# SSM exchange copied by GpSimd, SSM output written and loaded by halves, and other buffers for the FFN's first up weights

## The chip, the cores and the metric

The kernel runs on one core of a Trainium2 chip. What is measured is the device time of one execution, in microseconds (us); the time of a kernel is the median of its runs.

## The reference, cut to what matters

One layer of a hybrid encoder for a prompt of 1024 tokens and a sample of 64, width 1024. Both go through the same weights, so the kernel treats them as 1088 token columns.

```python
proj = rmsnorm(x) @ w_in                  # q, k, v, u, gate_attn, gate_ssm
o_attn = stick_breaking(q, k, v)          # 8 heads of 64
# S5: 32 groups of 16 channels, 64 complex states each
s[t] = lam * s[t-1] + B u[t];  y = Re(C s) + D u
y = gelu(y);  o_ssm = y * sigmoid(y @ w_glu)
merged = sigmoid(g_attn) * (o_attn @ w_branch_attn) + sigmoid(g_ssm) * (o_ssm @ w_branch_ssm)
x = x + rmsnorm(merged @ w_out)
f = (silu(f0 @ w_gate) * (f0 @ w_up)) @ w_down          # f0 = rmsnorm(x), 2816 wide
x = x + rmsnorm(f);  x = x + rmsnorm(sigmoid(rmsnorm(x) @ w_ple_gate) * (p @ w_ple_proj))
```

## The kernel before, in words

All products are made of split operands: a float32 matrix becomes a high part, rounded by a copy on ScalarE, and a low part, the difference on VectorE (`split` and `unit`, lines 106 to 126), and three matmuls make one product (lines 137 to 139).

The order on each engine and on each DMA queue is not written by hand here. The framework plans it from the order in which the program names its operations and from a simulated timeline (`schedule_with_timeline_sim=True`); on the chip each queue then runs strictly in that order. Nearly all DMAs are issued by SyncE (SP), a few by GpSimd.

**The SSM.** Time is cut into chunks of T = 8 steps: 128 chunks of the prompt, one empty column and 8 of the sample make NCH = 137 columns. Each group becomes two matmuls of 128x128 on 137 columns: a Toeplitz block `toep` on the inputs `ut` (line 571) and the table `cm` on the chunk states `hist` (line 572). Real and imaginary parts and the two halves of the groups lie on different halves of the partitions, so that `cm`, and later `hist`, has to be exchanged between partitions 0 to 63 and 64 to 127: `exchange` sends each half by DMA into `cx` (lines 542 and 543) and copies it back in place, one copy on ScalarE (line 544), one on VectorE (line 545). The chunk states come from a scan on VectorE, some hundred small steps (`cmul`, lines 271 to 277). `ssm_out` then does the matmuls of three groups into one bank, evicts it with a Gelu on ScalarE into `ut` (line 573), twelve evictions in all, the halves of the groups in turn. When all are done it writes `ut` to a DRAM tensor `ydr`, one DMA for each of the 8 steps (line 577), 16 partitions and 32 groups each. `glu` loads `ydr` back with the channels on the partitions, four tiles `y` of 128 channels (line 585), splits each into `ya`, and multiplies by `w_glu`, for each bank over k = 0, 1, 2, 3.

Beside the SSM TensorE has other work: the gate projections and parts of q, k and v (`fill`), which are made column by column in between, evicted by ScalarE (`gs`, line 909; two buffers) and stored to DRAM (line 910). Their weights are split at lines 119 and 115. In this stage the projections take three banks in turn.

**The FFN's start.** The FFN runs in 11 blocks of 256 columns. `wino_weights` loads two halves of a block's gate or up weights (line 1116) and splits them. For i even, the gate, the raw tile comes from the pool `W`, which is open all the time (tag `wraw`, two buffers); for i odd, the up weights, from the pool `ffn1`, tag `raw`, which is opened when the pool of the stage before (`mix`) is closed and lies over it. `ffn_first` treats block 0 in its own way: both weights are split first, and only their plain products are made (sums=False). Before it, `mix_out` finishes the tokens: a norm, transposes, and the stores of sums of token blocks to `tk` (line 1029), which `wino_tokens` loads again as `st` (line 1103).

The functions that the change touches, and what calls them:

Of the kernel before, what the change touches and what calls it, by code (L numbers as in the profile page):

```python
# [8 lines left out]
F32 = mybir.dt.float32  # L9
F32R = mybir.dt.float32r  # L10
BF = mybir.dt.bfloat16
AF = mybir.ActivationFunctionType
# [13 lines left out]
T = 8  # L26
NCH = SEQ // T + 1 + DEC // T
# [41 lines left out]
class Net:  # L69
# [464 lines left out]
                n = N // (2 * s)  # L534
                step(cols(b + s, 2 * s, n), cols(b, 2 * s, n), n, l)

    def exchange(self, x, T):

        nc, n = self.nc, x.shape[2] // 2
        for i, t in enumerate(T):  # L540
            v = x[:, :, i * n:(i + 1) * n]
            nc.sync.dma_start(t[64:], v[:64, 1])
            nc.sync.dma_start(t[:64], v[64:, 0])
            nc.scalar.activation(v[64:, 0], t[64:], AF.Copy)
            nc.vector.tensor_copy(v[:64, 1], t[:64])

    def ssm_out(self, Q, U):
        nc = self.nc
        V, hist = nc.vector, self.hist

        ps = self.ps.tile([128, 512], F32, name="tr", tag="tr")
        fin = Q.tile([16, 4, 128], F32, name="fin")
        fs = Q.tile([128, 4, 16], F32, name="fs")
        V.tensor_copy(fs[:, 0:2], hist[:, :, :, S0 - 1])
        V.tensor_copy(fs[:, 2:4], hist[:, :, :, NCH])
        X = [U.tile([128, T, NCH], F32, name="us", tag="us", bufs=2) for _ in range(2)]
        self.exchange(hist[:, :, :, :NCH], X)
        for i in range(4):
            nc.tensor.transpose(ps[:16, i * 128:(i + 1) * 128], fs[:, i], self.ident)
        V.tensor_copy(fin, ps[:16].rearrange("g (i s) -> g i s", i=4))  # L560
        for i, o in enumerate((4, 5, 8, 9)):
            nc.sync.dma_start(self.O[o][0, 0].rearrange("(h g) p -> g h p", h=2),
                              fin[:, i].rearrange("g (h p) -> g h p", h=2))
        self.ydr = self.dram.tile([512, T, NCH], F32, name="ydr")
        for g0 in [h * 16 + i for i in range(0, 16, 3) for h in range(2)]:
            w = min(3, 16 - g0 % 16)
            ps = self.ps.tile([128, 512], F32, name="z", tag="z")
            for j in range(w):
                h, g = divmod(g0 + j, 16)
                o = ps[:, j * NCH:(j + 1) * NCH]  # L570
                nc.tensor.matmul(o, self.toep[:, g0 + j].rearrange("p n c -> p (n c)"), self.ut[:, g0 + j], start=True, stop=False)
                nc.tensor.matmul(o, self.cm[:, h, g].rearrange("p n c -> p (n c)"), hist[:, h, g, :NCH], start=False, stop=True)
            nc.scalar.activation(self.ut[:, g0:g0 + w], ps[:, :w * NCH].rearrange("p (a n) -> p a n", a=w),
                                 AF.Gelu_apprx_tanh)
        dst = self.ydr.rearrange("(g c) t n -> t c g n", c=16)
        for t in range(T):
            nc.sync.dma_start(dst[t], self.ut[t * 16:(t + 1) * 16])

    def glu(self, P):

        nc = self.nc
        Y, YA, B = [], [], []
        for k in range(4):
            y = P.tile([128, T, NCH], F32, name="y", tag="y", bufs=4)
            nc.sync.dma_start(y, self.ydr[k * 128:(k + 1) * 128])
            ya = P.tile([128, 2, TOK], F32R, name="ya", tag="ya", bufs=4)
            for c0, n0, n in ((0, 0, SEQ // T), (SEQ, S0, DEC // T)):
                h, l = (ya[:, i, c0:c0 + n * T].rearrange("p (c t) -> p t c", t=T) for i in range(2))
                self.split(h, l, y[:, :, n0:n0 + n])
            Y.append(y)  # L590
            YA.append(ya)
        for m in range(4):
            s = P.tile([128, TOK], F32, name="sg", tag="sg", bufs=2)

            def evac(ci, c0, n, ps, s=s):
                nc.scalar.activation(s[:, c0:c0 + n], ps, AF.Sigmoid)
            self.fm_cols(self.I["w_glu"][0], m * 128, 4, evac, acts=YA)
            for c0, n0, n in ((0, 0, SEQ // T), (SEQ, S0, DEC // T)):
                v = s[:, c0:c0 + n * T].rearrange("p (c t) -> p t c", t=T)
                nc.vector.tensor_mul(v, v, Y[m][:, :, n0:n0 + n])  # L600
            if "o_ssm" in self.dbg:
                nc.sync.dma_start(self.dbg["o_ssm"][m * 128:(m + 1) * 128], s)
            b = P.tile([128, 2, TOK], F32R, name="bs", tag="bs", bufs=4)
            self.split(b[:, 0], b[:, 1], s)
            B.append(b)
        for m in range(8):
            g = P.tile([128, TOK], F32, name="gl", tag="gl", bufs=2)
            nc.sync.dma_start(g, self.gd[8 + m])

            def evac(ci, c0, n, ps, g=g):  # L610
                nc.vector.tensor_mul(g[:, c0:c0 + n], ps, g[:, c0:c0 + n])
            self.fm_cols(self.I["w_branch_ssm"][0], m * 128, 4, evac, acts=B)
            nc.sync.dma_start(self.gd[8 + m], g)
# [495 lines left out]
    def wino_weights(self, P, w, p, i, sums=True):  # L1109

        nc, W = self.nc, self.W
        G = nc.gpsimd
        raw, D = [], []
        for r in range(2):
            x = W.tile([128, 4, 256], F32, name="raw", tag="wraw", bufs=2) if i % 2 == 0 else P.tile([128, 4, 256], F32, "raw", "raw")
            nc.sync.dma_start(x, w[:, 4 * r:4 * r + 4, p * 256:(p + 1) * 256])
            if not sums and i == r == 1:
                h, l = (P.tile([128, 4, 256], F32R, n, "s") for n in ("wh", "wl"))
            elif (2 * i + r) % 3 < 2:
                h = W.tile([128, 4, 256], F32R, name="wh", tag="whi", bufs=2)  # L1120
                l = W.tile([128, 4, 256], F32R, name="wl", tag="wlo", bufs=2)
            else:
                h, l = P.tile([128, 4, 256], F32R, "wh", "dh"), P.tile([128, 4, 256], F32R, "wl", "dl")
            self.split(h, l, x)
            raw.append(x)
            D.append((h, l))
        if not sums:
            return D
        a11, a21 = (raw[0][:, :, s:s + 128] for s in (0, 128))
        a12, a22 = (raw[1][:, :, s:s + 128] for s in (0, 128))  # L1130

        def part(op, x, y):
            t = P.tile([128, 4, 128], F32, "st", "st")
            op(t, x, y)  # L1134
            s = P.tile([128, 2, 4, 128], F32R, "s", "s")
            self.split(s[:, 0], s[:, 1], t)
            return t, (s[:, 0], s[:, 1])
        _, s3 = part(G.tensor_sub, a11, a21)
        t1, s1 = part(G.tensor_add, a21, a22)
        t2, s2 = part(G.tensor_sub, t1, a11)  # L1140
        _, s4 = part(G.tensor_sub, a12, t2)
        h = lambda d, n: tuple(x[:, :, n * 128:(n + 1) * 128] for x in d)
        return D, dict(a11=h(D[0], 0), a12=h(D[1], 0), a22=h(D[1], 1), s1=s1, s2=s2, s3=s3, s4=s4)
# [327 lines left out]
def body(tc, I, O, dbg=None, upto=99):  # L1471
    with ExitStack() as ctx:
        N = Net(ctx, tc, I, O, dbg, upto)
        nc = tc.nc
# [3 lines left out]
        W = N.W = ctx.enter_context(tc.tile_pool(name="W", bufs=1))  # L1478
# [15 lines left out]
        def fill(n):  # L1494
            for _ in range(n):
                next(dense, None)

        def pool(name, side="left"):
            return tc.tile_pool(name=name, bufs=1, reuse_waits="tile", side=side)
# [6 lines left out]
        with pool("ssm") as PS:  # L1506
            with pool("tab") as PT:
                N.ssm_load(PT)
                for _ in range(4):
                    for x in two:  # L1510
                        next(x, None)
                PU = pool("u", "right")
                pu = PU.__enter__()
                N.u_proj(pu)
                with N.tc.issue_after(N.last_dve.ins), N.tc.issue_after(N.last_pool.ins):
                    N.ssm_tables(PS, PT)
                    N.ssm_chunks(PS)
                    N.ssm_response(PS, PT)
            with pool("toep") as P1:
                N.ssm_toeplitz(P1)  # L1520
                N.exchange(N.cm.rearrange("p r g n c -> p r g (n c)"), [P1.tile([128, 8, 128], F32, name=f"cx{i}") for i in range(2)])
                N.ssm_scan(pu)
                fill(3 * G1)
                N.ssm_out(P1, pu)
            PU.__exit__(None, None, None)
# [29 lines left out]
        with pool("wout", "right") as PW:  # L1555
            N.HS = PW.tile([128, 8, 2 * DEC], F32R, name="HS")
            with pools(tc, "mrgB", dict(braw=1, ga=2, gs=2)) as P:
                raw = mA[0].tile([128, TOK], F32, "braw", "braw")
# [46 lines left out]
```

## Time and profile before

| | us |
|---|---|
| median of 3 runs | 1780.83 (1775.21 to 1787.9) |
| profiled execution | 1778.77 |
| its span, from the first to the last instruction | 1776.6 |
| TensorE busy in the span | 1692.9 (95%) |
| VectorE, ScalarE, GpSimd busy | 1039.0, 733.5, 515.3 |

The span is what the trace covers; the execution's own time is a little longer. In the rows below, L and a number is a line of the kernel; PE is TensorE, ACT ScalarE, DVE VectorE, POOL GpSimd, SP SyncE. Times are from the span's start.

### The profile page before, as it was taken

Reading aid. Unit: us, or ns where it says so; the run is one execution under the profiler, and the core shown is the slowest. Engines: PE = TensorE matmul, PEld = TensorE weight load, DVE = VectorE, ACT = ScalarE, POOL = GpSimd, SP = SyncE. Lnnn points to the kernel's source line nnn. Section 1 sums busy time; section 2 is a strip of 40 time slices with the busy share of each in tenths; the row PEclk is TensorE's granted clock in tenths of the full one; section 3 lists DMA queues with packets and bytes.
Section 4 is the critical chain, followed back from the end, with each engine's and each line's share of the span. In section 5 each row is a group of like instructions: output and inputs, shape, how many; then the busy total and the mean of one; then the engine's idle time right before and its main releaser. Section 6 shows DMA issues by size and latency. Waiting matters only on the chain.

```text
span 1776.6 us, 24710 instructions
## 1 busy us (share of the span) xinstructions
PE 1692.9 (95%) x9092; PEld 1479.3 (83%) x9092; DVE 1039.0 (58%) x1581; ACT 733.5 (41%) x1357; POOL 515.3 (29%) x446
## 2 busy tenths in 40 slices
PE   8999897999999988899998999999999999999998
PEld 6999897988888877799786788888888887888886
DVE  6437735435776777767463655555655455445674
ACT  6431134124555555643343433343333344444542
POOL 2026100012322323224230444445444313001453
PEclk9999898999999999999999999999999999999999
DMA  8352534675343342147454444445444386655332
GB/s 283 95 147 64 120 89 149 216 213 137 88 101 101 83 118 83 60 143 239 143 172 148 132 149 133 160 132 187 151 149 139 125 288 215 197 189 166 107 113 89
DMA packets 220457, 258.23 MB, mean 145 GB/s; under 512 B 25888, under 2 KB 168336, under 8 KB 220320
## 3 DMA queue, kind: packets, MB, share of 16 engines
q1 hardware_dynamic: 219680, 255.20, 46.9%
q0 software_dynamic: 656, 1.44, 0.5%
q8 instruction: 72, 1.18, 0.3%
q14 instruction: 49, 0.40, 0.1%
HBM read 165.32 MB, written 76.51 MB: 136 GB/s over the span
## 4 chain that ended last, share of the span: by engine, by line
PE 73%; DVE 12%; DMA 7%; ACT 3%; issue 3%; SPq 1%; POOL 1%; DVEq 0%; POOLq 0%; ACTq 0%
PE pj L1200 13%; PE tr L1200 6%; PE pj L137 6%; PE pj L139 6%; PE pj L138 6%; PE z L1366 3%; DVE p L730 3%; PE z L1200 3%; PE pj L1366 3%; PE z L138 2%; PE z L139 2%; PE z L137 2%; PE tr L1366 2%; PE av L806 2%; PE tr L776 1%
## 5 line engine op out<-in xcount | busy, mean ns | idle before, releaser
L137 PE MATMUL pj<-H,wh 128*128 128x362 f32 (+3 forms) x648 | 217.7, 336 | 5.9 <-DVE ql L629 3.3
L139 PE MATMUL pj<-H,wl 128*128 128x362 f32 (+3 forms) x648 | 215.1, 333 | 0.6 <-DVE wl L115 0.6
L138 PE MATMUL pj<-H,wh 128*128 128x362 f32 (+3 forms) x648 | 214.6, 331 | 0.0
L126 DVE TENSOR_TENSOR wl<-raw,wh 128x1024 fp32r<-128x1024 f32 x96 | 132.3, 1380 | 120.0 <-ACT wh L125 118.7
L732 POOL TENSOR_TENSOR w<-w,p 128x383 f32<-128x383 f32 (+4 forms) x68 | 92.7, 1372 | 312.5 <-DVE w L734 185.2
L125 ACT ACTIVATE wh<-raw 128x1024 fp32r<-128x1024 f32 x96 | 101.4, 1059 | 122.8 <-PE z L1366 45.5
L137 PEld LDWEIGHTS pj<-H,wh 128*128 128x128 f32 x648 | 122.8, 190 | 7.6 <-DVE ql L629 3.7
L139 PEld LDWEIGHTS pj<-H,wl 128*128 128x128 f32 x648 | 122.5, 189 | 1.5 <-DVE wl L115 0.8
L138 PEld LDWEIGHTS pj<-H,wh 128*128 128x128 f32 x648 | 122.7, 189 | 0.9 <-issue 0.4
L1200 PE MATMUL pj<-H,s 128*128 128x512 f32 x480 | 118.2, 395 | 0.0
L148 POOL TENSOR_TENSOR rs<-rs,mhalf 128x1 f32<-128x1 f32 (+1 forms) x54 | 32.6, 605 | 278.0 <-DVE rs L147 277.9
L1200 PEld LDWEIGHTS pj<-H,s 128*128 128x128 f32 x480 | 89.9, 188 | 21.0 <-DVE c L1233 0.3
L125 ACT ACTIVATE s<-st 128x512 fp32r<-128x512 f32 x80 | 50.3, 629 | 123.6 <-PE pj L1200 112.2
L1134 POOL TENSOR_TENSOR st<-raw 128x512 f32<-128x512 f32 x40 | 60.7, 1518 | 133.8 <-DVE H L126 54.0
L126 DVE TENSOR_TENSOR s<-st,s 128x512 fp32r<-128x512 f32 x80 | 67.8, 849 | 39.4 <-ACT s L125 38.7
L119 ACT ACTIVATE wh<-raw 128x1024 fp32r<-128x1024 f32 (+1 forms) x52 | 46.8, 899 | 94.2 <-PE av L138 48.8
L780 ACT ACTIVATE wth<-tr 128x512 fp32r<-128x512 f32 (+2 forms) x112 | 50.2, 454 | 82.4 <-PE tr L776 41.9
L781 DVE TENSOR_TENSOR wtl<-tr,wth 128x512 fp32r<-128x512 f32 (+2 forms) x112 | 55.3, 496 | 49.3 <-ACT wth L780 48.9
L115 DVE TENSOR_TENSOR wl<-raw,wh 128x1024 fp32r<-128x1024 f32 (+1 forms) x50 | 51.1, 1021 | 55.0 <-ACT wh L119 54.9
L728 ACT ACTIVATE p<-z 128x512 f32<-128x512 f32 (+4 forms) x116 | 59.1, 510 | 42.6 <-PE z L830 16.7
L730 DVE TENSOR_TENSOR_SCAN p<-p,zero 128x384 f32<-128x384 f32 (+4 forms) x68 | 73.9, 1094 | 0.2
L1200 PE MATMUL pj<-H,wh 128*128 128x512 f32 x224 | 72.7, 401 | 0.6 <-ACT H L125 0.4
(553 smaller groups left out, 4630.2 us busy)
## 6 DMA issues: line engine op xcount, KB each, us to landing
sd<-c SPq DMA_DIRECT2D x77, 256.0 KB, 3.2
raw<-sd SPq DMA_DIRECT2D x77, 256.0 KB, 2.9
raw<-in_w_in_dram SPq DMA_DIRECT2D x32, 512.0 KB, 5.3
raw<-in_w_ffn_gate_dram SPq DMA_DIRECT2D x22, 512.0 KB, 3.6
raw<-in_w_ffn_up_dram SPq DMA_DIRECT2D x22, 512.0 KB, 5.1
wd<-in_w_ffn_down_dram SPq DMA_DIRECT2D x44, 256.0 KB, 3.3
td<-wd SPq DMA_DIRECT2D x22, 512.0 KB, 3.2
raw<-td SPq DMA_DIRECT2D x44, 256.0 KB, 3.0
```

The lines of the kernel that those rows point to most:

```text
L125: self.nc.scalar.activation(wh, raw, AF.Copy)
L126: self.nc.vector.tensor_sub(wl, raw, wh)
L137: self.nc.tensor.matmul(out, wh, xh, start=i == 0, stop=False)
L138: self.nc.tensor.matmul(out, wh, xl, start=False, stop=False)
L139: self.nc.tensor.matmul(out, wl, xh, start=False, stop=i == n - 1)
L728: nc.scalar.activation(p, z, AF.Sigmoid, scale=-1.0)
L730: nc.vector.tensor_tensor_scan(p[:, ::-1], p[:, ::-1], self.zero.to_broadcast([128, n]), 1.0 if carry is None else carry, op0=OP.mult, op1 ...
L732: (nc.gpsimd if e == 'g' else nc.vector).tensor_tensor(w[:, :n - 1], w[:, :n - 1], p[:, 1:], op=OP.mult)
L781: nc.vector.tensor_sub(wl[:, a:b], ps[:, a:b], wh[:, a:b])
L1134: op(t, x, y)
L1200: self.nc.tensor.matmul(out, a[i][:, k], b[j][:, k], start=start and k == i == j == 0, stop=stop and k == 3 and i == 1, skip_group_check=n ...
L1366: nc.tensor.matmul(B[b + n], x[:, 0, c], y[:, 1], start=new and p == j == 0, stop=p == 10 and j == 2, skip_group_check=not new)
```

## The change

Three things are changed. The exchange of `cm` gets both copies on GpSimd (the exchange of `hist` stays on ScalarE and VectorE). `ssm_out` works through the first 8 groups of each half and then the last 8, six evictions each, and after each six it writes what it has: 16 DMAs, for each step and each half of the groups, of 16 partitions and 8 groups; `glu` loads and splits the tiles in the order 0, 2, 1, 3 (0 and 2 hold the first part), and uses them in the order 0, 1, 2, 3 as before. And the raw tile of block 0's up weights comes from `W` with the gate's.

```diff
-    def exchange(self, x, T):
+    def exchange(self, x, T, engines=None):
...
+        e = engines or (nc.scalar.copy, nc.vector.tensor_copy)
...
-            nc.scalar.activation(v[64:, 0], t[64:], AF.Copy)
-            nc.vector.tensor_copy(v[:64, 1], t[:64])
+            e[0](v[64:, 0], t[64:])
+            e[1](v[:64, 1], t[:64])
...
-        for g0 in [h * 16 + i for i in range(0, 16, 3) for h in range(2)]:
-            w = min(3, 16 - g0 % 16)
...
-        dst = self.ydr.rearrange("(g c) t n -> t c g n", c=16)
-        for t in range(T):
-            nc.sync.dma_start(dst[t], self.ut[t * 16:(t + 1) * 16])
+        dst = self.ydr.rearrange("(h b g c) t n -> b t c h g n", h=2, b=2, c=16)
+        src = self.ut.rearrange("p (h b g) n -> p h b g n", h=2, b=2)
+        for b in range(2):
+            for i in range(0, 8, 3):
+                for h in range(2):
+                    w = min(3, 8 - i)
+                    g0 = h * 16 + b * 8 + i
...
+            for t in range(T):
+                for h in range(2):
+                    nc.sync.dma_start(dst[b, t, :, h], src[t * 16:(t + 1) * 16, h, b])
...
-        for k in range(4):
+        for k in (0, 2, 1, 3):
...
-            x = W.tile([128, 4, 256], F32, name="raw", tag="wraw", bufs=2) if i % 2 == 0 else P.tile([128, 4, 256], F32, "raw", "raw")
+            x = W.tile([128, 4, 256], F32, name="raw", tag="wraw", bufs=2) if i % 2 == 0 or not sums else P.tile([128, 4, 256], F32, "raw", "raw")
...
-                N.exchange(N.cm.rearrange("p r g n c -> p r g (n c)"), [P1.tile([128, 8, 128], F32, name=f"cx{i}") for i in range(2)])
+                N.exchange(N.cm.rearrange("p r g n c -> p r g (n c)"), [P1.tile([128, 8, 128], F32, name=f"cx{i}") for i in range(2)],
+                           [nc.gpsimd.tensor_copy] * 2)
```

## Rows read from the trace of the kernel before

**Rows 1.** TensorE's timeline: start, us, engine, line, names, shapes, count, idle before and releaser.

```profile
199.59 0.67 PE L137 MATMUL av<-H,wh 128*128 128x362 f32 x1 [7.25 <-ACT gs L909]
...
281.88 0.67 PE L137 MATMUL tr<-ya,wh 128*128 128x364 f32 x1 [9.02 <-ACT ya L125]
```

**Rows 2.** TensorE's waits from 935 to 1010: us in total, times, longest.

```profile
PE tr L1200 <- ACT wh L125: 4.9, 1, 4.9
```

**Rows 3.** Windows: us, busy by engine (xcount), granted clock, DMA share, GB/s.

```profile
185.00:190.00 5.00, 5.00 (x32) 5.00 (x31) 0.71 (x4) 0.00 (x0) 0.00 (x0) 1.00 1.08 172
...
200.00:205.00 5.00, 5.00 (x18) 5.00 (x18) 4.66 (x17) 0.47 (x1) 0.00 (x0) 0.50 0.68 206
...
280.00:285.00 5.00, 2.31 (x6) 1.84 (x7) 3.14 (x3) 5.00 (x5) 0.00 (x0) 0.50 1.03 413
285.00:290.00 5.00, 5.00 (x24) 5.00 (x24) 5.00 (x6) 4.98 (x7) 0.00 (x0) 0.74 0.35 131
...
960.00:965.00 5.00, 4.95 (x15) 4.00 (x16) 4.58 (x6) 3.42 (x6) 0.00 (x0) 0.66 0.55 179
```

**Rows 4.** ScalarE's timeline around the exchange of cm.

```profile
190.37 1.06 ACT L544 ACTIVATE cm<-cx 64x1024 f32<-64x1024 f32 x1 [9.42 <-DMA cx<-cm]
...
199.08 0.46 ACT L909 ACTIVATE gs<-av 128x362 f32<-128x362 f32 x1
```

**Rows 5.** VectorE's timeline there: its two copies of the exchange.

```profile
190.36 0.68 DVE L545 COPY cm<-cx 64x1024 f32<-64x1024 f32 x1 [4.58 <-DMA cx<-cm]
...
197.05 0.69 DVE L545 COPY cm<-cx 64x1024 f32<-64x1024 f32 x1 [5.25 <-DMA cx<-cm]
```

**Rows 6.** Timelines of GpSimd and VectorE: a GpSimd copy and steps beside it.

```profile
154.50 2.16 POOL L430 COPY cbd<-dc 64x512 f32<-64x512 f32 x2
...
154.53 1.65 DVE L276 TENSOR_TENSOR us<-us 128x1024 f32<-128x1024 f32 x1
156.22 1.52 DVE L277 TENSOR_TENSOR hist<-hist,us 128x1024 f32<-128x1024 f32 x1
...
162.32 1.22 DVE L277 TENSOR_TENSOR hist<-hist,us 128x1024 f32<-128x1024 f32 x1
```

**Rows 7.** The same two timelines in the FFN: a GpSimd operation with two inputs.

```profile
1002.40 1.62 POOL L1134 TENSOR_TENSOR st<-raw,st 128x512 f32<-128x512 f32 x1
...
1002.79 1.78 DVE L1255 TENSOR_TENSOR c<-c 128x512 f32<-128x512 f32 x1
...
1006.19 0.68 DVE L1256 TENSOR_TENSOR c<-c 128x512 f32<-128x512 f32 x1
```

**Rows 8.** SP's queue: writes and loads of the SSM's output, loads of its input.

```profile
257.73 12.78 SPq L577 DMA_DIRECT2D ydr<-ut  x8
...
275.58 2.02 SPq L585 DMA_DIRECT2D y<-ydr  x4
...
90.58 5.41 SPq L484 DMA_DIRECT2D ut<-udr  x8
...
102.51 3.63 SPq L484 DMA_DIRECT2D ut<-udr  x8
```

**Rows 9.** ScalarE's timeline: the sixth and the last eviction, first splits of ya.

```profile
249.39 0.52 ACT L573 ACTIVATE ut<-z 128x411 f32<-128x411 f32 x1 [0.89 <-PE z L572]
...
257.42 0.29 ACT L573 ACTIVATE ut<-z 128x137 f32<-128x137 f32 x1 [0.28 <-PE z L572]
...
279.79 4.04 ACT L125 ACTIVATE ya<-y 128x1024 fp32r<-128x1024 f32 x3 [3.22 <-DMA y<-ydr]
```

**Rows 10.** DMA issues: names, queue, count, KB each, median us to landing.

```profile
ut<-udr SPq DMA_DIRECT2D x32, 68.5 KB, 3.2
```

**Rows 11.** ScalarE's timeline at the FFN's start: the first split of up weights.

```profile
958.94 1.06 ACT L125 ACTIVATE wh<-raw 128x1024 fp32r<-128x1024 f32 x1 [6.88 <-DMA raw<-in_w_ffn_up_dram]
```

**Rows 12.** SP's queue: the loads of the first gate and up weights.

```profile
849.52 8.85 SPq L1116 DMA_DIRECT2D raw<-in_w_ffn_gate_dram  x4
...
953.06 1.41 SPq L1116 DMA_DIRECT2D raw<-in_w_ffn_up_dram  x2
```

More of the change, by code (lines that the diff above doesn't have):

```diff
@@ L564, in ssm_out @@
         self.ydr = self.dram.tile([512, T, NCH], F32, name="ydr")
-        for g0 in [h * 16 + i for i in range(0, 16, 3) for h in range(2)]:
-            w = min(3, 16 - g0 % 16)
[L567 to L574, printed above, removed]
-        dst = self.ydr.rearrange("(g c) t n -> t c g n", c=16)
-        for t in range(T):
-            nc.sync.dma_start(dst[t], self.ut[t * 16:(t + 1) * 16])
+        dst = self.ydr.rearrange("(h b g c) t n -> b t c h g n", h=2, b=2, c=16)
[5 more added lines that the diff above has]
+                    g0 = h * 16 + b * 8 + i
+                    ps = self.ps.tile([128, 512], F32, name="z", tag="z")
+                    for j in range(w):
+                        o = ps[:, j * NCH:(j + 1) * NCH]
+                        g = b * 8 + i + j
+                        nc.tensor.matmul(o, self.toep[:, g0 + j].rearrange("p n c -> p (n c)"), self.ut[:, g0 + j], start=True, stop=False)
+                        nc.tensor.matmul(o, self.cm[:, h, g].rearrange("p n c -> p (n c)"), hist[:, h, g, :NCH], start=False, stop=True)
+                    nc.scalar.activation(self.ut[:, g0:g0 + w], ps[:, :w * NCH].rearrange("p (a n) -> p a n", a=w),
+                                         AF.Gelu_apprx_tanh)
+            for t in range(T):
+                for h in range(2):
+                    nc.sync.dma_start(dst[b, t, :, h], src[t * 16:(t + 1) * 16, h, b])
     def glu(self, P):
         nc = self.nc
-        Y, YA, B = [], [], []
-        for k in range(4):
+        Y, YA, B = [None] * 4, [None] * 4, []
+        for k in (0, 2, 1, 3):
             y = P.tile([128, T, NCH], F32, name="y", tag="y", bufs=4)
@@ L589, in glu @@
                 self.split(h, l, y[:, :, n0:n0 + n])
-            Y.append(y)
-            YA.append(ya)
+            Y[k], YA[k] = y, ya
         for m in range(4):
```

## The prediction

> **What bounds the kernel now.** I read the page first: TensorE is busy 95% of the span, so only stretches where it stands still, or runs at its lower clock, are worth anything. The list of TensorE's waits, stage by stage, comes next, and its timeline where the list has a long one. Around the SSM there are two: 7.3 us for an eviction of the gate projections (ACT gs), up to 199.59, and 9.0 us for the first split of the SSM's output (ACT ya), up to 281.88 [rows 1]. At the start of the FFN one stands out, 4.9 us for a weight split (ACT wh) [rows 2]. The windows table then shows what each costs behind itself: TensorE's granted clock is 1.00 (2.4 GHz) before the first of them and 0.50 (1.2 GHz) in the five us after it, with 18 matmuls where 32 of the same kind fit; 0.50 and 0.74 after the second; 0.66 after the third [rows 3]. Last, the timelines of the queues that stand in front of the three waits. Each part of the change touches one of them.
>
> **Part 1: the table's exchange on GpSimd.** Now ScalarE and VectorE each hold, in order, two copies of cm that wait for a DMA from another half of the partitions. ScalarE waits 9.42 us ahead of the first; the gate eviction due behind it runs only at 199.08 [rows 4], so TensorE runs out of banks. VectorE waits 4.58 and 5.25 us and copies for 0.68 and 0.69 [rows 5]: 11.2 us, and all of it is in the SSM's scan, whose small steps stand behind the copies.
> Removed for TensorE: 7.3 us of standing still, and the low clock after it, (32 - 18) x 5/32 = 2.2 us [rows 1, 3]: 9.5 us. Removed for the scan: 11.2 us. The matmuls of the SSM's output need both, so the smaller counts.
> Added: four copies of 64x1024 on GpSimd. The nearest row is its copy of 64x512, two in 2.16 us [rows 6], so one of 1024 is 2.16 us and the four 8.6 us. GpSimd has nothing else there: its busy time is 0.00 in the stretches on both sides [rows 3], and nothing is queued behind that would be needed soon. The table is first read by the SSM's output matmuls; of their twelve evictions the sixth runs at 249.39, 50 us behind the copies [rows 9], which is the cover; without it the four copies would add their 8.6 us.
> They do meet VectorE. While the two 64x512 copies ran, a VectorE step of 128x1024 took 1.65 us and the one behind it, half beside them, 1.52; soon after, without them, such a step took 1.22 [rows 6]. That is 0.73 us of VectorE for 2.16 us of GpSimd, so 2.9 us for 8.6. The other end is a GpSimd operation with two inputs: during one of 1.62 us a VectorE step took 1.78 us instead of 0.68 [rows 7]; at worst VectorE stands for all 8.6 us. I take 2.9, from the row that is a copy as well.
> So the scan gains 11.2 - 2.9 = 8.3 us (2.6 at worst), TensorE's own side 9.5; the part gives **8.3 us**, 2.6 to 9.5.
> The Trainium skill's page SBUF — State Buffer (Summary: rules for kernel authors) speaks against this part: a VectorE instruction with two SBUF inputs and a GpSimd one that reads SBUF block each other fully. The two-input rows agree with it, the copy rows show a third of it; by that rule this part would give 2.6 us.
> A store of gate columns that is issued behind the cx transfers will still land late. I cost that at nothing: an eviction has two buffers, and TensorE three banks of 24 matmuls each, 11 us at 32 in 5 us [rows 3]; that cover gone, TensorE would wait again, which the bounds hold.
>
> **Part 2: the SSM's output by halves.** The matmuls and Gelus now run to 257.7; only then are eight writes issued, in 12.78 us, and the loads of y start at 275.58; the first split runs at 279.79 [rows 8, 9]. TensorE resumes at 281.88, at half clock [rows 1]. From 280 to 290 it does 6 + 24 matmuls [rows 3]; at full speed, 0.156 us each, 30 matmuls would have ended at 290 had they begun at 285.3. That is the mark to compare with.
> After the change everything up to the Gelus is 8.3 us earlier. The first half is done after the sixth of twelve evictions, 249.91 - 8.3 = 241.6, the second at 249.4 [rows 9]. The writes are then 32 of 68.5 KB. Operations of just this shape and size are in the trace, the loads of ut: eight issues took 5.41 and 3.63 us (the other two sets lie between), 0.45 to 0.68 each, and a landing takes 3.2 us [rows 8, 10]. I take 0.55. The first sixteen go out by 241.6 + 8.9 = 250.5, beside the second half's matmuls; the next sixteen by 259.3; landed 262.5. The load of y takes 4.2 us (275.58 to 279.79), the split 1.06 on ScalarE [rows 11] and about 1.2 on VectorE. glu's matmuls take k in the order 0, 1, 2, 3, and k = 1 is of the second half: its first part is there at 262.5 + 4.2 + 1.1 = 267.8.
> TensorE has filling work until its wait begins; that was 9.0 us ahead of 281.9, at 272.9 [rows 1], and becomes 264.6, to which the nine matmuls of k = 0 add 1.4. It waits 1.8 us, and I add 1 for VectorE's part and the clock. Equivalent start: 267.8 - 1.4 + 1 = 267.4.
> One thing is not shown by the trace: the order on SP. The loads of y 0 and 2 wait for the first half's writes to land. Placed ahead of the second half's writes they hold them, and the column stores queued with them, for the 3.2 us of a landing and two more issues, and the longer wait costs clock: about 5 us, a start at 272.4. Which one the planner chooses can't be read from before; I take the middle, 270.
> Parts 1 and 2 together: 285.3 - 270 = **15.3 us**, between 12.9 and 17.9 by SP's order, and down to 7 with part 1 at its worst. The reordering of k among the loads costs nothing: the same splits, all before k = 1.
>
> **Part 3: the up weights.** The gate's two loads run at 849.52, and with them those of the next block's gate weights, four in all, because their buffers come from the pool that is open all the time. The first up weights have buffers of a pool that lies over the one before it: they are issued at 953.06, behind the stores of the last tokens, and split at 958.94 [rows 11, 12]. TensorE waits 4.9 us for that split [rows 2].
> With the gate's buffers the loads can go out where the next block's gate loads went, and land about 90 us early. The price: those gate loads come after the up splits, but they are needed only after all of the first block's products. The split still needs room in the pool that opens there, so it can't be as early as the load.
> Removed: 4.9 us and the clock, (1 - 0.66) x 5 = 1.7 us [rows 3]: 6.6 us. If the split's own room is late, nothing. The token loads behind the up loads start at the same stores as before, so a little may come back: I take **6 us**, 0 to 6.6.
>
> **The sum.** 15.3 + 6 = 21.3. The profiled execution took 1778.77 us, 2.2 of them outside its span: 1757.5. It lies 2.1 us below the median of the three runs, so I say 1758. The stages between and after are bound by TensorE, so the shift passes through.
>
> **The rivals.**
> - *GpSimd takes VectorE's time.* The scan gains 2.6, SP holds the second half: 12.9 - 5.7 = 7.2, with part 3 13.2: 1766. For it: rows 7. Against: rows 6, and that VectorE's steps there are short. 0.16.
> - *The up weights' split is late anyway*, for its room or its place on ScalarE: 1778.8 - 15.3 = 1763.5. For it: the row shows only that the load came last, not when the room was free. Against: ScalarE stands idle ahead of it. 0.14.
> - *Slower: a write costs by its count, not by its bytes.* SP took 1.6 us for each of the eight writes [rows 8]. If that were the price of an issue, 32 take 51 us: 241.6 + 51.1 + 3.2 + 4.2 + 1.1 = 301.2, 16 us behind the mark of 285.3; with part 3's 6 back, 10 us slower: 1789. It decides from about 1.2 us an issue. Against: the loads of ut, 0.45 to 0.68. 0.05.
> The page DMA: Bandwidth & Descriptors of the Trainium skill (Anatomy of one DMA — SWDGE (gpsimd) path) gives each DMA about 2.0 us whatever its size; one behind the other 32 would be an estimated 64 us. The ut rows speak against paying that in series.
> - *The change doesn't do what it says:* the planner writes every queue anew, the up loads stay behind the token stores, or an early split of y stands on ScalarE ahead of an eviction, as the cm copies did. Part of the 21 us then comes back as another wait: 1766 to 1780. 0.12.
>
> **How the numbers follow.** The forecast has 0.53, with its own range 1751 to 1764 (part 1 at 9.5, SP's better order and 6.6 make about 1753). All these cases but the slower one lie between 1750 and 1780; leaving out some of the fourth and the slower one, and keeping the median's own scatter below, the range is 1747 to 1776. About 1% (17.8 us, so 1763) is what a measurement of this kernel can tell from no change. The forecast is nearly all beyond it, the first two rivals a few us on this side of it: faster 0.58, same 0.37; slower by 1% needs the third rival and a replanned queue: 0.05.
>
> **What would show it.** Right: no wait of TensorE for gs near 192 and a clock of 1.00 through 200; the copies of cm on GpSimd, VectorE's scan without its two holes; the last Gelu at about 249 instead of 257; writes of ydr in two runs, the first beside the matmuls; TensorE's wait for ya at most 5 us; the up loads where four gate loads are now, and no wait for wh at the FFN's start. Wrong: VectorE steps lengthened to 2 us beside GpSimd; writes at over 1 us an issue; loads of y between the two runs of writes; ScalarE standing for y with evictions behind it; another wait of like length a few us after one that is gone.

## The result, and the profile after

The changed kernel takes 1769.57 us (median of 9 runs, 1766.16 to 1772.19), the kernel before 1781.46 beside it: ratio 0.9924, 95% interval 0.991 to 0.9938, some 13.5 us. The gain is clear of noise, under 1%, and smaller than the forecast: 1758 was said, 1747 to 1776 was the range.

The list of TensorE's waits around the SSM, after:

```profile
PE tr L560 <- DVE fs L556: 3.1, 1, 3.1
PE tr L138 <- DVE ya L126: 2.3, 2, 1.4
PE tr L560 <- DVE fs L555: 1.6, 1, 1.6
PE tr L137 <- ACT ya L125: 0.3, 1, 0.3
```

Both waits of [rows 1] are gone: none for gs, and ya is down from 9.0 us to 0.3 for ScalarE's part, while VectorE's part of it went from 0.8 us to 2.3. What has grown is the wait for the transposes of the final states (fs), which stand in TensorE's queue and need the scan. Before, it was 1.6 us:

```profile
PE tr L559 <- DVE fs L555: 1.6, 1, 1.6
```

After, it is 3.1 and 1.6 us, and the granted clock, 1.00 in the five us ahead, is down with it (columns as in [rows 3]):

```profile
220.00:225.00 5.00, 2.67 (x10) 2.59 (x11) 4.55 (x24) 0.00 (x0) 0.00 (x0) 0.62 0.38 127
225.00:230.00 5.00, 5.00 (x24) 5.00 (x23) 0.53 (x1) 1.06 (x1) 0.00 (x0) 0.70 0.69 151
```

GpSimd's timeline, and VectorE's beside it:

```profile
186.67 1.05 POOL L545 COPY cm<-cx 64x1024 f32<-64x1024 f32 x1 [8.25 <-DMA cx<-cm]
187.77 1.04 POOL L546 COPY cm<-cx 64x1024 f32<-64x1024 f32 x1
188.76 4.89 POOL L461 DMA_DIRECT2D toep<-kd  x8
193.69 1.93 POOL L545 COPY cm<-cx 64x1024 f32<-64x1024 f32 x1
195.67 1.66 POOL L546 COPY cm<-cx 64x1024 f32<-64x1024 f32 x1
```

```profile
186.63 0.22 DVE L271 TENSOR_TENSOR us<-hist,sq 128x32 f32<-128x32 f32 x1
186.76 1.03 DVE L272 TENSOR_TENSOR us<-hist,sqi 128x32 f32<-128x32 f32 x1
187.83 1.05 DVE L276 TENSOR_TENSOR us<-us 128x32 f32<-128x32 f32 x1
...
194.69 1.78 DVE L271 TENSOR_TENSOR us<-hist,sq 128x512 f32<-128x512 f32 x1
196.40 0.96 DVE L555 COPY fs<-hist 128x32 f32<-128x32 f32 x1
```

The copies take 5.7 us in all, 1.05 and 1.04 in the first pair, 1.93 and 1.66 in the second, which meets larger VectorE steps. The two small steps beside the first pair take 1.03 and 1.05 us where their neighbour takes 0.22. The planner also put the first pair ahead of the eight issues of toep, so these wait with GpSimd for cx. The queue of SP, before and after, shows what comes out: the exchange of hist, which ends the scan, starts 8.3 us earlier. (About 0.5 us of it is there ahead of the exchange of cm: a gate eviction that starts at 180.47 before starts at 179.96 after.)

```profile
233.29 0.63 SPq L542 DMA_DIRECT2D us<-hist  x1
```

```profile
224.97 0.63 SPq L543 DMA_DIRECT2D us<-hist  x1
...
241.02 8.40 SPq L583 DMA_DIRECT2D ydr<-ut  x16
...
250.14 7.62 SPq L583 DMA_DIRECT2D ydr<-ut  x16
...
260.61 2.17 SPq L591 DMA_DIRECT2D y<-ydr  x4
```

The writes go out in two runs, 0.53 and 0.48 us an issue; all four loads of y stand behind both, at 260.61 against 275.58 [rows 8]. The first sigmoid of glu, on ScalarE, is a mark that both kernels have. Before:

```profile
292.39 0.48 ACT L596 ACTIVATE sg<-tr 128x364 f32<-128x364 f32 x1 [2.06 <-PE tr L139]
```

and after:

```profile
278.45 0.48 ACT L601 ACTIVATE sg<-tr 128x364 f32<-128x364 f32 x1 [3.28 <-PE tr L139]
```

13.9 us earlier. So parts 1 and 2 came nearly as forecast; the rest is at the FFN's start. TensorE's waits there, after:

```profile
PE z L1196 <- DVE y L1193: 8.9, 1, 8.9
...
PE tr L1205 <- DVE wl L126: 0.3, 1, 0.3
```

The 4.9 us for wh [rows 2] are gone, and 8.9 us for y stand in their place, the input of the transposes of the sample's gated rows. That wait was there before too, in the line below the one in [rows 2]:

```profile
PE z L1191 <- DVE y L1188: 2.8, 1, 2.8
```

The windows of that stretch after (columns as in [rows 3]):

```profile
960.00:965.00 5.00, 0.00 (x0) 0.00 (x0) 2.62 (x4) 1.89 (x3) 0.00 (x0) 0.68 0.70 226
965.00:970.00 5.00, 1.51 (x5) 1.20 (x6) 2.81 (x6) 2.93 (x6) 0.00 (x0) 0.50 0.75 223
```

TensorE does nothing for these five us, and its granted clock is 0.68 in them and 0.50 in the next five. SP's queue and ScalarE's timeline show why:

```profile
843.53 2.73 SPq L1121 DMA_DIRECT2D raw<-in_w_ffn_up_dram  x2
...
945.04 0.93 SPq L1121 DMA_DIRECT2D raw<-in_w_ffn_up_dram  x2
946.02 1.29 SPq L1121 DMA_DIRECT2D raw<-in_w_ffn_gate_dram  x2
948.01 10.59 SPq L1108 DMA_DIRECT2D st<-tk  x5
```

```profile
937.42 2.01 ACT L125 ACTIVATE wh<-raw 128x1024 fp32r<-128x1024 f32 x2
...
956.24 1.94 ACT L125 ACTIVATE T<-st 128x512 fp32r<-128x512 f32 x3 [5.30 <-DMA st<-tk]
961.14 1.30 ACT L125 ACTIVATE T<-st 128x512 fp32r<-128x512 f32 x2 [2.96 <-DMA st<-tk]
963.08 0.63 ACT L125 ACTIVATE T<-st 128x512 fp32r<-128x512 f32 x1 [0.64 <-DMA st<-tk]
965.66 1.28 ACT L125 ACTIVATE T<-st 128x512 fp32r<-128x512 f32 x2 [1.94 <-DMA st<-tk]
966.84 0.36 ACT L978 ACTIVATE q<-av 64x256 f32<-64x256 f32 x1
```

The up loads go out at 843.53 and are split at 937.42 as the change wants. But q, the first step from the sample's product to its transposes, is queued on ScalarE behind the splits of the token sums (T), and each of those waits for its load. Counted from the first load of token sums (954.93 before, 943.65 after), TensorE came to the transposes after 25.9 us before and after 15.9 in the changed kernel, but y was ready after 28.7 and 24.8: TensorE gained 10 us on that load, y only 4.

### The profile page after: what moved, and what is told of

Read it like the earlier page. It is cut to its first block, busy times and chain, and to the rows that moved or that the text cites. A ratio compares the mean times of both kernels' runs of the same rounds, so it can differ in the third digit from the quotient of the medians.

```text
span 1766.7 us, 24728 instructions
## 1 busy us (share of the span) xinstructions
PE 1692.9 (96%) x9092; PEld 1478.4 (84%) x9092; DVE 1041.0 (59%) x1579; ACT 731.2 (41%) x1355; POOL 522.3 (30%) x450
## 4 chain that ended last, share of the span: by engine, by line
PE 72%; DVE 13%; DMA 6%; ACT 3%; issue 3%; POOL 1%; SPq 1%; DVEq 0%; POOLq 0%; ACTq 0%
PE pj L1205 13%; PE tr L1205 6%; PE pj L137 6%; PE pj L139 6%; PE pj L138 6%; PE z L1371 3%; DVE p L735 3%; PE z L1205 3%; PE pj L1371 3%; PE tr L1371 2%; PE av L811 2%; PE z L138 2%; PE z L139 2%; PE z L137 2%; PE tr L781 1%
```

## Experiments

Theory A: parts 1 and 2 give the whole gain; part 3 gives none, since TensorE then waits at the transposes, whose input stands behind the token splits on ScalarE. Rival B: part 3 gave its us, and the loss is in the attention, whose queues were planned anew. All ratios are to the kernel before, run beside the kernel in question.

**The parts by themselves.** Part 3 alone is this line in the kernel before:

```diff
-... if i % 2 == 0 else P.tile([128, 4, 256], F32, "raw", "raw")
+... if i % 2 == 0 or not sums else P.tile([128, 4, 256], F32, "raw", "raw")
```

> Only the up weights' buffers are changed. Theory A (the wait for the up split is replaced, a few us later, by a wait of TensorE for the sample's transposes, whose input stands on ScalarE behind the token splits): no gain, ratio 0.998 to 1.002 to the kernel before; TensorE's wait for wh of 4.9 us gone, its wait for y grown from 2.8 to about 9 us. Rival B (part 3 does give its 4 to 6 us, and the missing part of the forecast was lost in the attention, whose queues were planned anew): ratio about 0.997, and the wait for y stays near 3 us.

Ratio 1.0006 (0.9995 to 1.0017). TensorE's waits at the FFN's start in it:

```profile
PE z L1191 <- DVE y L1188: 10.6, 1, 10.6
```

Theory A holds: the wait for wh is no longer listed, the one for y is 10.6 us.

The same line taken out of the changed kernel:

> The change without the up weights' buffers. Theory A: the same time as the whole change, 0.992 to the kernel before. Rival B: 4 to 6 us slower than the whole change, 0.995.

Ratio 0.9902 (0.9886 to 0.9919): as fast as the whole change or some 4 us faster (the intervals overlap a little), with the two waits of before back:

```profile
PE tr L1205 <- ACT wh L125: 4.7, 1, 4.7
PE z L1196 <- DVE y L1193: 2.5, 1, 2.5
```

B falls. Then parts 1 and 2 apart, `exchange` on GpSimd with `ssm_out` and `glu` of before, and the reverse:

> Only the exchange of the table on GpSimd. By the prediction's first part the SSM's output starts 8.3 us earlier and nothing behind it changes: 0.9953 to the kernel before, and TensorE's wait for the first split of ya stays near 9 us. Rival (the late stores of gate columns and the shorter scan only move TensorE's wait to the transposes of the final states): under 4 us, 0.998.

Ratio 0.9938 (0.9923 to 0.9952), 11 us, more than forecast; the wait for ya stays:

```profile
PE tr L137 <- ACT ya L125: 10.3, 1, 10.3
```

> Only the output by halves. By the prediction's second part about 7 us, 0.996 to the kernel before, with the wait for gs near 192 still at 7 us and the wait for ya down from 9 to under 3 us. Rival (the two parts need each other, since the writes of the first half only help when TensorE's filling work lasts as long): under 3 us alone.

Ratio 0.9958 (0.9944 to 0.9973), 7.5 us; the wait for ya falls to 1.6 and 1.9 us, the one for gs stays, longer than before:

```profile
PE av L137 <- ACT gs L913: 10.1, 1, 10.1
```

11 and 7.5 make 18.5, and both together gave 17.5 (e2): within these intervals the two add up and don't need each other.

**What holds part 3 back.** The whole change, with the gating and the transposes of the sample's up rows named after the products of both token blocks:

```diff
                     self.decode_rows(Q, self.decode_pairs(HD, D[up]), 0, 16)
-                    self.decode_gate(P, Q, up, 0)
+                    if not up:
+                        self.decode_gate(P, Q, up, 0)
                 self.wino_tokens(PT, P, False)
+        self.decode_gate(P, Q, 1, 0)
```

> The whole change, and block 0's sample rows of the up weights are gated and transposed only after the products of both token blocks, so that TensorE passes no transposes there that wait for ScalarE. Theory A (part 3's gain is held by these transposes alone): the wait of 8.9 us is gone, 5 to 8 us faster than the whole change, 0.987 to 0.989 to the kernel before. Rival C (the token splits are late for all that follows, so TensorE waits at the next block instead): within 2 us of the whole change, 0.992.

> The same with the up weights' buffers as before the change. Theory A: TensorE waits 4.7 us for wh and nothing behind it; part 3 is then worth its 4.7 us and the clock, so this is 4 to 6 us slower than with it. Rival C: the same time as with it.

With part 3 the ratio is 0.9874 (0.986 to 0.9888), clear of the whole change's; without it 0.9886 (0.9871 to 0.9901). The longest waits of TensorE there, first with part 3, then without:

```profile
PE pj L1207 <- DVE c L1233: 2.3, 1, 2.3
```

```profile
PE tr L1207 <- ACT wh L125: 5.1, 1, 5.1
```

So the 8.9 us were the transposes' place in the queue: 9 us by the runs (0.9924 to 0.9874). Without part 3, where the wait was 2.5 us, the same move gave 2.9 us (0.9902 to 0.9886). What theory A said of part 3 itself, 4 to 6 us once the transposes are out of the way, is only half shown. The runs with and without part 3 differ by 2 us, with intervals that overlap. Two marks on SP, the loads of the gains at the start and at the end of the stage, give it more exactly, with part 3:

```profile
826.01 0.38 SPq L955 DMA_DIRECT2D gb_norm_ffn_pre<-in_norm_ffn_pre_dram  x1
...
1422.01 0.42 SPq L955 DMA_DIRECT2D gb_norm_ffn_post<-in_norm_ffn_post_dram  x1
```

and without:

```profile
822.73 1.91 SPq L955 DMA_DIRECT2D gb_norm_ffn_pre<-in_norm_ffn_pre_dram  x1
...
1422.75 0.42 SPq L955 DMA_DIRECT2D gb_norm_ffn_post<-in_norm_ffn_post_dram  x1
```

596.0 us against 600.0. That is one profile of each; two more kernels with both edits (e12 and e9 below) have 597.1 and 598.5 between these marks, so 1.5 to 4 us is what can be said.

Why are the token splits late? The whole change with the next block's weight loads held behind the last token load (`issue_after` that load), and, in another kernel, five buffers for the token loads (`st=3` becomes `st=5`):

> The whole change, with the next block's four weight loads put behind the last of the twelve token loads in SP's queue. Theory D (what makes the splits late is those 2 MB between the third and the fourth token load): TensorE's wait for y falls from 8.9 to 3 to 5 us, 4 to 6 us faster than the whole change, 0.989. Rival (the splits are late since each load waits for one of three buffers): the wait stays above 7 us and the time at 0.992, or worse if the next block's weights now come too late.

> The whole change with five buffers instead of three for the token loads. Theory D: the fourth and fifth load can go ahead of the weight loads or together with them; the wait for y falls by 1 to 4 us. Rival (three buffers are what binds): it falls to 3 us or less and the time to 0.988.

Ratios 0.9903 (0.9891 to 0.9916) and 0.9922 (0.9905 to 0.9938). The waits, first with the loads held, then with five buffers:

```profile
PE z L1199 <- DVE y L1196: 7.8, 1, 7.8
```

```profile
PE z L1196 <- DVE y L1193: 8.0, 1, 8.0
```

As the whole cause both theories fall: each edit alone takes about 1 us off the wait. By time the first is perhaps 4 us ahead of the whole change, the second not at all, and both intervals overlap with its own. The twelve loads start only when the last token's sums are stored; counted from the first of them y is ready after 24.8 us in the whole change, 24.1 with the loads held and 23.6 with five buffers. What would shorten that stays open. The held loads together with the transposes moved:

> The transposes of the sample rows moved, and the next block's weight loads behind the token loads. If the token splits are on the path at the next block: 2 to 4 us faster than with the transposes moved alone, 0.985 to 0.986. If they are not: the same, 0.987.

0.9864 (0.9848 to 0.9881), 1761.09 us: not to be told from e5's. The token splits are not on the path once no transposes wait for what stands behind them. With e5 this is the best version found, 9 to 11 us under the change and 5 to 7 under parts 1 and 2 alone (e2).

**What bounds the SSM's output now.** Each write cut in two, for the same bytes:

```diff
-                    nc.sync.dma_start(dst[b, t, :, h], src[t * 16:(t + 1) * 16, h, b])
+                    for q in (slice(0, 4), slice(4, 8)):
+                        nc.sync.dma_start(dst[b, t, :, h, q], src[t * 16:(t + 1) * 16, h, b, q])
```

> The whole change with each of the 32 writes of the output cut into two of 4 groups, 64 in all, the same bytes. If a write is priced by its bytes: the two runs of issues keep their 8 us each and the time stays at 0.992. If by its count, 0.5 us each: each run takes 16 us, glu starts 10 to 16 us later, and the gain of the halves is gone, 0.998 to 1.001.

0.9955 (0.9939 to 0.997), 5.5 us slower than the change, where 10 to 16 had been expected of a price by count. SP's queue and the wait it makes:

```profile
237.57 33.07 SPq L584 DMA_DIRECT2D ydr<-ut  x64
```

```profile
PE tr L137 <- ACT ya L125: 11.5, 1, 11.5
```

33.07 us for 64, 0.52 each, as for twice the size. Between these two sizes a write is priced by its count; not so up to the four times larger writes of before, at 1.6 us [rows 8]. In its profile glu's first sigmoid comes 11.8 us later than in the change's, and why the runs lose only half of that was not followed.

The order of the loads of y, 0, 1, 2, 3 as before:

> The whole change with y loaded and split in the order 0, 1, 2, 3 as before. By the prediction the order costs nothing: 0.992. Rival (the early loads of k = 0 and 2 are what lets the splits start while the second half is written): ya later by two splits, 2 to 3 us slower.

0.9908 (0.9889 to 0.9927): no difference that can be told, as all four loads stand behind both runs of writes anyway.

The transposes of the final states named behind the output (on top of e5):

> The kernel with the transposes of the sample rows moved (0.9874 to the kernel before), and also the four transposes of the final states put behind the SSM's output, so that TensorE no longer waits 1.5 and 3.2 us for the scan there. Theory E (the chain through the scan and the output now sets when glu can start, TensorE's filling work just covers it): the waits come back as a longer wait for ya, no gain, 0.986 to 0.989. Rival (TensorE's own work is the bound there): 5 to 8 us, with the clock, 0.983 to 0.985.

0.9872 (0.9855 to 0.989), the same as e5. But it didn't test the theory: the planner left the transposes where they were. The pair that waits longest runs at 221.02, 9 us ahead of the output's first matmul on hist (at 230.09), and in e5 at 222.87, as far ahead of it (231.97); TensorE's wait is the same.

```profile
PE tr L579 <- DVE fs L555: 3.1, 1, 3.1
```

Whether the scan's chain or TensorE's own work is the bound there stays open.

## Why the prediction was right, and where it wasn't

The range held, and so did the sign; the gain was about six tenths of the forecast (13.5 us of 22.8), and one term is to blame, part 3. (1.5 us of the 22.8 are in no term: the sum of 21.3 was taken from the profiled execution, 2.1 us under the median.) That parts 1 and 2 came close is in part luck.

*Part 1.* The scan was to gain 8.3 us, and in the profile after, the exchange of hist starts 8.3 us earlier. But other profiles spread around that pair: in the three kernels without part 1 (before, e1, e4) the exchange starts at 233.29, 234.37 and 235.82, in the eleven with it between 223.68 and 225.51, 9.8 us apart in the mean. By itself the part gave 11 us, with an interval that reaches down to 8.6. The term removed was the smallest of three: VectorE's two holes and copies are 11.2 us before, 12.3 in e1 and 14.0 in e4, where the waits for cx were 5.21 and 7.42. The term added, 2.9 us, was hit by two errors that cancel. The first is a reading of [rows 6], whose 2.16 us for two copies merge these:

```profile
154.50 0.60 POOL L430 COPY cbd<-dc 64x512 f32<-64x512 f32 x1
155.14 1.52 POOL L430 COPY cbd<-dc 64x512 f32<-64x512 f32 x1
```

The later one ends 0.48 us after VectorE's step beside it, which ran to 156.18; that step, begun 0.03 us after the first copy, took 1.65 us instead of 1.23. So each engine seems to have waited for the other in turn: a copy of 64x512 takes some 0.6 us, and one of 64x1024 took 1.05, not 2.16. The second error is that beside a copy VectorE stands for nearly all of it, not for a third. The four steps shown lost about 0.8, 0.8, 0.7 and 0.75 us (against 0.22, 0.22, about 1.1 and 0.2 undisturbed), 3.0, where 2.9 was said; and the second pair of copies lost 1.5 us to VectorE's steps. The Trainium skill's rule in SBUF — State Buffer (Summary: rules for kernel authors), full blocking of whichever comes second, agrees with the small steps: one starts 0.09 us after a copy of 1.05 and takes 1.03. It agrees with the two copies of [rows 6] as well, where the prediction saw only a third of it. What was wrong in the 2.6 us that the prediction made of it is the length of the copies, and that VectorE stands for all of it: only the steps that meet a copy are held.

- *The late stores of gate columns*, costed at nothing: ScalarE did wait for them (4.32 us ahead of 201.09), TensorE didn't. What was not foreseen is toep's eight issues behind the first two copies on GpSimd; it costs nothing seen here.
- *Part 2.* Issues of 0.53 and 0.48 us against 0.55 said; SP's order was the better of the two; k = 1 did not wait for loads in between. Parts 1 and 2 were to give 15.3 us; glu's first sigmoid came 13.9 earlier, and e2 gave 17.5 (14.5 to 20.3). The 13.9 is one pair of profiles: with neither part the sigmoid stands at 292.39 and 296.06 (before, e1), with both, and writes of 68.5 KB, between 275.14 and 280.17.
- *Part 3 failed*, at the sentence that a wait removed gives 4.9 us and the clock, 6 us in all. It gave nothing (e1). The step left out is what is late next: TensorE had a second wait in that stage, 2.8 us for the sample's y, some 20 us behind the first, and its releaser did not depend on the up weights but on token loads that start with the last token's stores. With the first wait gone the second was 6.1 us longer in the change and 7.8 in e1. The fourth rival had this shape, another wait in the place of the one removed, but put it on evictions and on the up loads; the last of the signs of being wrong, another wait behind one that is gone, did appear.
- *The third rival* was right about a price by count, between 34 and 68.5 KB, with the wrong size: 0.5 us, not 1.6. At 32 writes the first run of them is hidden beside the matmuls; at 64 the writes cost 5.5 us more.
- Of the 13.9 us at the first sigmoid some 12 are left at the start of the FFN's norms. That was not followed further: two profiles with the same opening (before and e1) differ by more, e1's first sigmoid being 3.7 us behind.

## What to carry to other kernels

When a wait is to be removed, look at the next wait in the same stage and at what releases it: if that releaser doesn't move with the engine, the gain is only moved there. A step that reads a result late, like an eviction behind other work in an in-order queue, belongs to the critical path as soon as its reader is early enough; moving the reader took a few lines here and gave 9 us (2.9 without part 3). A merged row of a profile can hide that one of its operations was held: look at each before pricing by their mean. And cutting transfers in pieces to start earlier pays only while the issues are hidden: count them.

## What was not expected of the hardware

- A DMA of 16 partitions and pieces of 548 bytes costs SP about 0.5 us at 34 KB (64 in 33.07 us) as at 68.5 KB (16 in 8.40 and 7.62 us). At 274 KB it was 1.6 us [rows 8]. The Trainium skill's page DMA: Bandwidth & Descriptors (Anatomy of one DMA — SWDGE (gpsimd) path) gives about 2.0 us fixed for each DMA issued from GpSimd. No run here shows that for these writes, which SP issues: they take 2.7 us from issue to landing in the median at 68.5 KB and 1.8 at 34, and with an issue every 0.5 us they overlap.
- GpSimd copies 64x1024 in 1.05 us when both sides lie in a row, and 64x512 written in blocks of 16 in 0.60, when it comes first.
- VectorE and GpSimd hold each other. A VectorE step of 0.22 us is stretched to the length of the GpSimd copy that it meets, 1.03 us, though it moves only 32 elements a partition; a GpSimd copy of 1.05 us becomes one of 1.93 beside VectorE steps of 128x512.
